# Head norms of a hybrid decoder layer: sums of squares as four column strips instead of two full matmuls, and two inverse products put into one PSUM bank

## The chip, the cores and the metric

One Trainium2 chip; the program runs on one of its cores. The metric is the device time of one execution in microseconds (us), lower is better. The engines are named as in the profile: PE is TensorE (matmuls), PEld its weight loads, DVE is VectorE, ACT is ScalarE, POOL is GpSimd, and SP is the queue from which nearly all DMAs are issued.

## The reference, cut to what matters

One decoder layer, 2048 tokens, width 1024, all in float32. A combined projection feeds two groups of four heads of width 128: gated DeltaNet heads ("g") and HGRN2 heads ("h"). Every head's output is normed over its 128 channels and gated; then come the output projection, an MLP and a gated embedding, each with RMSNorms.

```
def gated_head_norm(o, w, z):
    o = o * lax.rsqrt(jnp.mean(o * o, axis=-1, keepdims=True) + EPS)
    return o * w.astype(jnp.float32) * jax.nn.silu(z)
...
        o_a = gated_delta_rule_chunked(q_a, k_a, v_a, g_dec, beta)
        o_a = gated_head_norm(o_a, gdn_norm[i], z_gdn)
...
        o_b = hgrn2_chunked(jax.nn.silu(q_hg), k_b, i_hg, log_f)
        o_b = gated_head_norm(o_b, hgrn_norm[i], g_hg)
```

The chunked delta rule solves a triangular system per chunk of the sequence; the kernel builds the inverse of that triangle from 32x32 blocks upward. Two of the products on that way are called `psx5` and `pst5` below.

## The kernel before, in words

Channels stand on the 128 partitions and tokens in the free dimension. The tokens go in four quarters `q` of 512 (`QT`), each of four chunks of 128. The large products keep float32 accuracy by splitting both operands into two parts of type fp32r and adding three products of the parts, each a 128x512 matmul.

The first stage (projections and mixers) runs over `works`: for each quarter one small projection (`ab`) and 32 projections of 24 matmuls each (8 for each of the four head pairs). A work is cut into three **ticks** of eight 128x512 matmuls (`SPT = 3`), so a head pair spans 24 ticks and a quarter 99. All the small work of the heads hangs on these ticks: a head is a generator, and a table of tick offsets (`A_STEPS` for g heads, `B_STEPS` for h heads, `A_LAST` and `B_LAST` for the last pair) says in which tick, counted from its pair's first work, each step up to the next `yield` is emitted. A half offset (`half()`) is a place in the middle of a tick. PE's order is the order of emission, and in this stage SP's is too, so an SP instruction that waits holds up all that stand behind it. The orders of DVE and ACT are set by the scheduler of the framework.

Inside a head PE runs two kinds of small float32 matmuls between the 128x512 ones: full ones (128x128 weights, 128 columns moving: `psa`, `psb`, `psc`, transposes `t_`) and **strips** (`strip`, 32 weight columns at `tile_position=(0, 32 g)`, four of which fill the array side by side: `psp`, `psx`, `pst`, `psd`, `at_all`, the small ones on `of_h` and `of_g`). A float32 matmul stands in the trace as two records, an fp32r one as a single record.

The norm of a head (`finish`, then `norm_steps`): ACT squares the output into `osq`, ACT and DVE split that into the two fp32r parts of `hl`, PE multiplies both by a matrix of ones (two 128x512 matmuls into one bank, `nrm`), so every row of the bank holds the sums; ACT copies row 0 out (1x512), and one row goes to DRAM (`sd`), back as 128x4 (`m`), through DVE and POOL (the -0.5 power), to DRAM (`rd`), and back spread over all partitions (`rsb`). DVE scales the output (`og`) and SP stores it (`mixd`). There are 32 such norms, 16 of g and 16 of h heads. `norm_steps` also serves the four embedding norms (`nrm_e`).

The PSUM pool `pp` of the mixers has three banks that all these small products take in turn.

Of the kernel before, what the change touches and what calls it, by code (L numbers as in the profile page):

```python
# [10 lines left out]
F32 = mybir.dt.float32  # L11
# [3 lines left out]
AF = mybir.ActivationFunctionType  # L15
# [5 lines left out]
P = 128  # L21
# [3 lines left out]
QT = 512  # L25
NQ = T // QT
NC = QT // P
# [4 lines left out]
SB = 32  # L32
# [22 lines left out]

A_STEPS = ((3, 6, 7, 8, 9, 10, 12, 14) + tuple(range(16, 24)) + (24, 26, 28, 30, 32, 34, 36)
           + tuple(o for c in range(38, 54, 4) for o in (c, c + 1.5, c + 2.5))
           + (53, 55, 57, 59, 60, 61, 65, 66))
I_STEPS = (22,)
B_STEPS = (24, 26, 28, 30, 32, 34, 36, 38, 40, 42, 44, 45, 46, 48, 50, 52, 53, 54, 58, 59)  # L60


A_AHEAD = (-12, -6)
# [2 lines left out]
A_FIRST = (3, 7, 8, 8, 9, 10, 12, 14) + tuple(range(16, 24)) + (24, 26, 29, 32, 34, 36, 37)  # L66

A_LAST = (A_STEPS[:16] + (24, 25, 27, 28, 29, 30, 31) + tuple(range(32, 44))
          + (44, 47, 49, 50, 51, 52, 54, 55))
B_LAST = tuple(range(24, 34)) + (35, 36, 37, 39, 41, 42, 43, 44, 46, 47)  # L70
LAST = 44


# [23 lines left out]
def trunk(ctx, tc, x, xT, pT, vecs, w_in, w_ab, gdn_a_log, gdn_dt_bias, w_out, w_up, w_down,  # L97
          w_ple, w_gate, consts, out):
    nc = tc.nc
    V, S, G, PE = nc.vector, nc.scalar, nc.gpsimd, nc.tensor  # L100
# [36 lines left out]
    def col(r):  # L137
        return cols[:, r : r + 1]
# [27 lines left out]
    ones = cp.tile([P, P], F32R, name="ones")  # L166
# [4 lines left out]
    def rsqrt(v):  # L171
        G.tensor_tensor(v, v, mhalf, ALU.pow)

    def split(t, eng, raw):

        S.activation(t[:, 0], raw, AF.Copy)  # L176
        eng.tensor_tensor(t[:, 1], raw, t[:, 0], ALU.subtract)  # L177
# [56 lines left out]
    def squares(acc, src, k, name, eng=V):  # L234

        if acc is None:
            acc = st.tile([P, QT], F32, tag="acc", name=f"acc_{name}", bufs=3)
            S.activation(acc, src, AF.Square)
        else:
            turns[0] += 1  # L240
            if pair[0] and turns[0] % 2:
                sq = st.tile([P, QT], F32, tag="late", name=f"sq_{name}_{k}")
            else:
                sq = st.tile([P, QT], F32, tag="sq", name=f"sq_{name}_{k}", bufs=1)
            S.activation(sq, src, AF.Square)  # L245
            eng.tensor_tensor(acc, acc, sq, ALU.add)  # L246
        return acc
# [7 lines left out]
    def spread_load(rd, name, pool=None, tag="rsb", bufs=2):  # L255
        rsb = (pool or st).tile([P, QT], F32, tag=tag, name=f"rsb_{name}", bufs=bufs)
        nc.sync.dma_start(rsb, rd.broadcast_to([P, QT]))
        return rsb
# [15 lines left out]
    yod = {q: [dr.tile([P, QT], F32, name=f"yod{q}_{d}") for d in range(KD)] for q in (0, 2, 3)}  # L274
    ple_r = [None] * NQ

    def norm_steps(acc, scale, eps, name, done, pool=None):

        hl = st.tile([P, 2, QT], F32R, tag="hl", name=f"hl_{name}", bufs=1)
        split(hl, V, acc)  # L280
        yield
        ps = bank(f"nrm_{name}", pool or pp)
        PE.matmul(ps, ones, hl[:, 0, :], start=True, stop=False)
        PE.matmul(ps, ones, hl[:, 1, :], start=False, stop=True)
        row = acc[0:1, :]
        S.activation(row, ps[0:1, :], AF.Copy)
        sd = dr.tile([1, QT], F32, name=f"sd_{name}")
        nc.sync.dma_start(sd, row)
        yield
        m = sm.tile([P, NC], F32, tag="m", name=f"m_{name}")  # L290
        nc.sync.dma_start(m, sd.rearrange("o (p n) -> (o p) n", n=NC))
        yield
        V.tensor_scalar(m, m, scale, eps, ALU.mult, ALU.add)
        rsqrt(m)
        yield
        rd = dr.tile([1, QT], F32, name=f"rd_{name}")
        nc.sync.dma_start(rd.rearrange("o (p n) -> (o p) n", n=NC), m)
        done(rd)
# [91 lines left out]
    with ExitStack() as ectx:  # L390
        es = ectx.enter_context(tc.tile_pool(name="es", bufs=1))
        with tc.manual_schedule(engines={mybir.EngineType.SP, mybir.EngineType.Activation, mybir.EngineType.DVE}):
# [44 lines left out]
            done = []  # L437
# [23 lines left out]
    with mixers as mctx:  # L461
# [145 lines left out]
        def finish(q, h, pso, zt, extra, eps, n):  # L607

            og = st.tile([P, QT], F32, tag="late", name=f"og_{n}")
            sq = st.tile([P, QT], F32, tag="acc", name=f"osq_{n}", bufs=3)  # L610
            S.activation(sq, pso, AF.Square, scale=P ** -0.5)
            V.tensor_tensor(og, pso, zt, ALU.mult)
            if extra is not None:
                V.tensor_tensor(sq, sq, extra, ALU.add)
            rd = []
            yield from norm_steps(sq, 1.0, eps, n, rd.append)
            yield
            rsb = spread_load(rd[0], n)
            yield
            V.scalar_tensor_tensor(og, og, col(R_GNORM if h < 4 else R_HNORM), rsb, ALU.mult, ALU.mult)  # L620
            yield
            nc.sync.dma_start(mixd[q][h], og)
# [10 lines left out]
        def gdn_mixer(q, h, live):  # L633

            n = f"g{q}_{h}"
# [8 lines left out]
            both = sm.tile([P, 2, NC], F32, tag="tail", name=f"tail_{n}")  # L644
# [41 lines left out]
            for c in range(0, NC, 2):  # L686
                ps = (of_h if c else of_g).rearrange("p (a b i) -> p a b i", a=2, b=2)
# [44 lines left out]
            for part_m, part_i in ((slice(SB // 4, SB // 2), slice(SB // 2, SB)), (slice(0, SB // 4), slice(0, SB))):  # L732
                width = part_i.stop - part_i.start
                t = fix[:, :, :width]
# [36 lines left out]
            def pair_bank(name):  # L771
                return bank(f"{name}_{n}", pp)[:, : QT // 2].rearrange("p (a i) -> p a i", a=2)

            def half_bank(name):
                return bank(f"{name}_{n}", pp)[:, : QT // 4].rearrange("p (a i) -> p a i", a=2)

            psp = half_bank("psp5")
            for p in range(2):  # L780
                for g in range(NB):
                    strip(g, psp[rows_of(g), p, rows_of(1 - g % 2)], um[5][:, p, rows_of(g)],
# [2 lines left out]
                S.activation(part[5][rows_of(g), :, rows_of(g ^ 1)], psp[rows_of(g), :, rows_of(0 if g % 2 else 1)],  # L785
                             AF.Copy)
            yield
            psx, pst = half_bank("psx5"), half_bank("pst5")
            for p in range(2):
                for g in range(NB):  # L790
                    strip(g, pst[rows_of(g), p, rows_of(g % 2)], part[5][:, p, rows_of(g)],
# [9 lines left out]
            psp = pair_bank("psp6")  # L801
# [352 lines left out]
        with tc.manual_schedule(engines={mybir.EngineType.SP}):  # L1154
# [5 lines left out]
            for j, (name, key, src, q, h, then, g, b) in enumerate(works):  # L1160
# [3 lines left out]
                ps = bank(f"mm_{name}")  # L1164
# [25 lines left out]
    pp = ctx.enter_context(tc.tile_pool(name="pq", bufs=4, space=PSUM))  # L1190
# [264 lines left out]
    for j, (q, d) in enumerate(order):  # L1455
# [32 lines left out]
        if j in held:  # L1488
            ps = held.pop(j)
        elif order[j] == TOGETHER[0]:  # L1490
# [5 lines left out]
            ps = held.pop(j)  # L1496
        else:
            ps = bank(f"mmo_{q}_{d}", pp)
# [3 lines left out]
        acc = square_sums[q] = squares(square_sums[q], ps, d, f"o{q}")  # L1502
# [403 lines left out]
    for half in range(2):  # L1906
# [4 lines left out]
        for d in range(KD):  # L1911
# [6 lines left out]
            for s, q in enumerate(qs):  # L1918
# [3 lines left out]
                ps = bank(f"mmg_{q}_{d}", pp)  # L1922
# [4 lines left out]
                t = es.pop((q, d))  # L1927
# [55 lines left out]
```

## Time and profile before

| what | value |
|---|---|
| median of 3 runs | 2637.18 us (2633.91 to 2642.8) |
| the profiled execution | 2643.16 us, span 2641.4 us |
| PE, DVE, ACT, POOL busy | 2601.6, 1964.7, 1464.2, 137.2 us |
| granted clock of TensorE | 1.00 |
| first stage in the trace | to about 1060 us of the span |

The busy time of PE counts a matmul until its modelled end, which lies behind the start of the next one, so the distance between starts, not the duration, tells what a matmul costs in a stream. "Idle before" an instruction starts at that modelled end too. A `PE ... <- X` in the views below means that PE's idle time ended when X released it.

### The profile page before, as it was taken

What the parts mean: (1) busy time and instruction counts of PE and PEld (TensorE: products, weight loads), DVE (VectorE), ACT (ScalarE), POOL (GpSimd) and SP (SyncE); (2) the same over time, 40 slices, a digit from 0 to 9 for tenths busy, and PEclk for the clock granted to TensorE, in tenths of its full rate; (3) what the DMA queues carried; (4) which work ended last, traced back from release to release, by engine and by line L of the source; (5) the groups of instructions that cost most, each with busy time, mean ns of one, the idle gap of its engine ahead of it and who ended that gap; (6) DMA issues with size and microseconds to landing.
All of it is one profiled execution on the core that took longest, in us unless ns stands there. A gap on an engine that the chain in (4) does not pass through costs nothing.

```text
span 2641.4 us, 43911 instructions
## 1 busy us (share of the span) xinstructions
PE 2601.6 (98%) x15593; PEld 2143.3 (81%) x15593; DVE 1964.7 (74%) x4032; ACT 1464.2 (55%) x2991; POOL 137.2 (5%) x147
## 2 busy tenths in 40 slices
PE   8999999999999999999999999999999999999999
PEld 5788788878878888787888888888888888888887
DVE  7788777776777777578988778767877765477776
ACT  7675655465555555566566465555455465565322
POOL 0000000000000000110000000001000001101000
PEclk9999999999999999999999999999999999999999
DMA  8777777767767675774675576665644375677664
GB/s 278 276 266 259 253 264 247 239 215 253 242 201 250 228 233 165 222 211 142 216 230 185 183 231 221 214 211 187 220 151 168 138 245 188 200 253 251 204 218 134
DMA packets 267788, 573.87 MB, mean 217 GB/s; under 512 B 55578, under 2 KB 60152, under 8 KB 250416
## 3 DMA queue, kind: packets, MB, share of 16 engines
q1 hardware_dynamic: 265264, 566.86, 64.5%
q0 software_dynamic: 2304, 4.20, 0.9%
q8 instruction: 123, 2.02, 0.3%
q14 instruction: 97, 0.79, 0.1%
HBM read 410.57 MB, written 160.37 MB: 216 GB/s over the span
## 4 chain that ended last, share of the span: by engine, by line
PE 76%; DMA 10%; DVE 7%; ACT 3%; issue 3%; SPq 1%; POOL 0%; DVEq 0%; ACTq 0%; POOLq 0%
PE d L1208 23%; PE u L1208 23%; PE mm L1174 17%; PE mmg L1208 7%; DMA cache_in<-w 2%; DMA sys_g<-ud_g 1%; PE mme L203 1%; DMA ud_g<-u_g 1%; DMA raw_out<-in_w_out_dram 1%; DMA mixT<-mixd 1%; DMA xs<-in_x_dram 1%; DMA yod<-yo 1%; DVE w L177 1%; DVE pr_g L744 0%; DMA wd<-in_w_down_dram 0%
## 5 line engine op out<-in xcount | busy, mean ns | idle before, releaser
L1174 PE MATMUL mm<-xt,w 128*128 128x512 f32 x3072 | 785.6, 401 | 2.6 <-DVE acc_vg L569 1.3
L1174 PEld LDWEIGHTS mm<-xt,w 128*128 128x128 f32 x3072 | 552.6, 188 | 109.1 <-ACT w L176 1.7
L1208 PE MATMUL d<-db,da 128*128 128x512 f32 x2688 | 612.8, 389 | 0.0
L1208 PE MATMUL u<-t,wu 128*128 128x512 f32 x2604 | 591.2, 389 | 0.0
L1208 PEld LDWEIGHTS d<-db,da 128*128 128x128 f32 x2688 | 504.5, 188 | 104.8
L1208 PEld LDWEIGHTS u<-t,wu 128*128 128x128 f32 x2604 | 488.7, 188 | 101.5
L230 DVE TENSOR_TENSOR db<-db 128x512 fp32r<-128x512 f32 x224 | 159.5, 712 | 62.0 <-ACT db L229 60.9
L1606 DVE TENSOR_TENSOR u<-u,u 128x512 f32<-128x512 f32 x224 | 150.5, 683 | 52.7 <-PE u L1208 51.2
L229 ACT ACTIVATE db<-db 128x512 fp32r<-128x512 f32 x224 | 140.9, 629 | 69.1 <-DMA db<-hid 66.7
L1208 PE MATMUL mmg<-h2T,wg 128*128 128x512 f32 (+1 forms) x792 | 174.7, 383 | 0.0
L1208 PEld LDWEIGHTS mmg<-h2T,wg 128*128 128x128 f32 x792 | 145.5, 188 | 29.1
L1649 ACT ACTIVATE u<-u 128x512 f32<-128x512 f32 x128 | 80.8, 631 | 155.0 <-DVE u L1606 154.5
L177 DVE TENSOR_TENSOR da<-da 128x512 fp32r<-128x512 f32 x128 | 94.5, 738 | 91.8 <-ACT da L176 89.9
L176 ACT ACTIVATE da<-da 128x512 fp32r<-128x512 f32 x128 | 80.6, 630 | 129.0 <-DMA da<-sumd 110.9
L1208 PE MATMUL mmo<-mixT,w_out 128*128 128x512 f32 x600 | 138.9, 391 | 3.6 <-DVE w_out L177 1.6
L1208 PEld LDWEIGHTS mmo<-mixT,w_out 128*128 128x128 f32 x600 | 112.1, 188 | 29.4 <-DVE w_out L177 2.9
L176 ACT ACTIVATE wu<-a 128x512 fp32r<-128x512 f32 x124 | 75.1, 623 | 53.3 <-DMA a<-in_w_up_dram 51.5
L177 DVE TENSOR_TENSOR wu<-a,wu 128x512 fp32r<-128x512 f32 x124 | 86.0, 695 | 8.0 <-ACT wu L176 7.5
L177 DVE TENSOR_TENSOR da<-dr,da 128x512 fp32r<-128x512 f32 x96 | 68.3, 711 | 22.4 <-ACT da L176 21.0
L1650 ACT ACTIVATE u<-u 128x512 f32<-128x512 f32 x128 | 80.4, 628 | 3.0
L246 POOL TENSOR_TENSOR acc_y<-acc_y,sq_y 128x512 f32<-128x512 f32 x28 | 37.6, 1341 | 759.9 <-ACT sq_y L245 759.9
L176 ACT ACTIVATE da<-dr 128x512 fp32r<-128x512 f32 x96 | 60.5, 630 | 29.4 <-DMA dr<-in_w_down_dram 21.1
(401 smaller groups left out, 3677.2 us busy)
## 6 DMA issues: line engine op xcount, KB each, us to landing
w<-cache_in SPq DMA_DIRECT2D x96, 1024.0 KB
db<-hid SPq DMA_DIRECT2D x224, 256.0 KB
cache_in<-w SPq DMA_DIRECT2D x32, 1024.0 KB
hid<-u SPq DMA_DIRECT2D x128, 256.0 KB
da<-sumd SPq DMA_DIRECT2D x128, 256.0 KB
a<-in_w_up_dram SPq DMA_DIRECT2D x124, 256.0 KB
hid<-ht SPq DMA_DIRECT2D x96, 256.0 KB
dr<-in_w_down_dram SPq DMA_DIRECT2D x96, 256.0 KB
```

The costliest lines, as they stand in the source:

```text
L176: S.activation(t[:, 0], raw, AF.Copy)
L177: eng.tensor_tensor(t[:, 1], raw, t[:, 0], ALU.subtract)
L203: PE.matmul(ps, a, b, start=i == 0, stop=i == n - 1)
L229: S.activation(t[:, 0], plain(t), AF.Copy)
L230: V.tensor_tensor(t[:, 1], plain(t), t[:, 0], ALU.subtract)
L246: eng.tensor_tensor(acc, acc, sq, ALU.add)
L1174: PE.matmul(ps, *terms[i], start=i == 0, stop=i == nt - 1)
L1208: PE.matmul(ps, a, b, start=start, stop=stop)
L1606: V.tensor_tensor(c[new], c[old], ps, ALU.add)
L1649: S.activation(c[k], c[k], AF.Relu)
L1650: S.activation(c[k], c[k], AF.Square)
```

## The change

The 32 head norms no longer split the squares. `norm_in_strips` takes the unsplit float32 squares: for each of the four chunks of 128 tokens one matmul with 32 columns of ones as weights, at column strip `c`, so that the sums of chunk `c` stand in partitions 32c to 32c+31 of a 128x128 area. ACT copies that area (128x128) in place of a row of 512; the DMA `sd` takes one partition of each strip (4x128). The rest of the chain is as before. The embedding norms keep the old way (`norm_whole`).

The chain has one step more, since `sd` is now issued in a tick of its own, and the tables move it. Counted in ticks of its pair, a g head now runs squares at 53, matmuls and copy at 56, `sd` 57, `m` 59, power 61, `rd` 62, `rsb` 63, scaling 67, `mixd` 68 (before: 53, all of 55, 57, 59, 60, 61, 65, 66). An h head: 46, 52, 53, 55, 57, 58, 59, 63, 64 (before: 46, all of 48, 50, 52, 53, 54, 58, 59). The last pair ends in the same ticks as before.

Second, `psx5` and `pst5`, two half-used banks before, become two areas of one bank (`half_banks`).

```
-           + (53, 55, 57, 59, 60, 61, 65, 66))
+           + (53, 56, 57, 59, 61, 62, 63, 67, 68))
...
-    def norm_steps(acc, scale, eps, name, done, pool=None):
+    def norm_in_strips(acc, name):
+
+        yield
+        ps = bank(f"nrm_{name}", pp)[:, :P]
+        for c in range(NC):
+            PE.matmul(ps[c * SB : (c + 1) * SB, :], ones.bitcast(F32)[:, :SB], acc[:, blk(c)], start=True, stop=True,
+                      tile_position=(0, c * SB))
+        S.activation(acc[:, :P], ps, AF.Copy)
+        sd = dr.tile([1, QT], F32, name=f"sd_{name}")
+        yield
+        nc.sync.dma_start(sd.rearrange("o (c n) -> (o c) n", n=P), acc[::SB, :P])
+        yield
+        return sd
+
+    def norm_whole(acc, name, pool):
 
         hl = st.tile([P, 2, QT], F32R, tag="hl", name=f"hl_{name}", bufs=1)
         split(hl, V, acc)
...
+    def norm_steps(acc, scale, eps, name, done, pool=None, strips=False):
+
+        sd = yield from norm_in_strips(acc, name) if strips else norm_whole(acc, name, pool)
...
-            yield from norm_steps(sq, 1.0, eps, n, rd.append)
+            yield from norm_steps(sq, 1.0, eps, n, rd.append, strips=True)
...
-            def half_bank(name):
-                return bank(f"{name}_{n}", pp)[:, : QT // 4].rearrange("p (a i) -> p a i", a=2)
+            def half_banks(name, count):
+                t = bank(f"{name}_{n}", pp)[:, : count * QT // 4]
+                return t.rearrange("p (m a i) -> m p a i", m=count, a=2)
 
-            psp = half_bank("psp5")
+            psp = half_banks("psp5", 1)[0]
...
-            psx, pst = half_bank("psx5"), half_bank("pst5")
+            both = half_banks("psx5", 2)
+            psx, pst = both[0], both[1]
```

PE's queue at the norm of the first h head (quarter 0, head 0), before; `mm` are the projections, `x3` counts matmuls in a row:

```order
L1174 MATMUL mm_0_2_1914<-xt_1_481,w_0_2_1744 128x512 x2
L1174 MATMUL mm_0_2_1914<-xt_2_498,w_0_2_1744 128x512 x2
L283 MATMUL nrm_h_0_1927<-hl_h_0_1879,ones 128x512
L284 MATMUL nrm_h_0_1927<-hl_h_0_1879,ones 128x512
L1174 MATMUL mm_0_2_1914<-xt_2_498,w_0_2_1744 128x512
```

The norm stood by itself between projections. The same norm on PE now:

```order
L1195 MATMUL mm_0_2_1986<-xt_5_547,w_0_2_1829 128x512
L282 MATMUL nrm_h_0_2008<-osq_h_0_1875,ones 32x128 x4
L650 MATMUL of_h<-att_h_1_1925,one 32x4x16 x4
L650 MATMUL at_all<-hb_h_1_1926,qk_h_1_1658 32x2x16 x16
L1195 MATMUL mm_0_2_1986<-xt_5_547,w_0_2_1829 128x512 x2
```

It has moved by four ticks and stands directly ahead of the first strips of the next h head. PE's queue at the norm of the first g head, before (`t_kg` are transposes of the head after next):

```order
L1174 MATMUL mm_0_2_2093<-xt_5_547,w_0_2_1907 128x512
L283 MATMUL nrm_g_0_2144<-hl_g_0_2073,ones 128x512
L284 MATMUL nrm_g_0_2144<-hl_g_0_2073,ones 128x512
L599 MATMUL t_kg_2_2153<-cst,y_kg_2_1990 128x128 x4
L1174 MATMUL mm_0_2_2093<-xt_5_547,w_0_2_1907 128x512 x2
```

There it stood ahead of four full float32 matmuls. The same norm on PE now (`psx` is the name of both inverse products):

```order
L1195 MATMUL mm_0_2_2082<-xt_7_566,w_0_2_1903 128x512 x3
L282 MATMUL nrm_g_0_2163<-osq_g_0_2062,ones 32x128 x4
L650 MATMUL psx_g_1_2170<-xt_g_1_1963,part_586 32x32 x4
L650 MATMUL psx_g_1_2170<-part_586,xt_g_1_1963 32x32 x2
L650 MATMUL psx_g_1_2170<-xt_g_1_1963,part_586 32x32 x4
L650 MATMUL psx_g_1_2170<-part_586,xt_g_1_1963 32x32 x2
L650 MATMUL at_all<-qk_h_1_1658,keys_h_1_2_2113 32x2x16 x8
```

It has moved by one tick, to the head of the run of strips with the next g head's inverse products. Of the 32 norms 23 stand like these two, in a run of strips between the projections' matmuls; 7 stand alone between projections (mostly those of a quarter's fourth pair, which the `ab` projection shifts against the next quarter), and 2 stand beside full 128x128 matmuls.

SP's queue around the second pair of quarter 0, before (`raw` and `cache_in` move the projections' weights, `xd` and `xn` carry the inverse's 32x32 blocks to DRAM and back):

```order
L192 DMA cache_in_2683<-w_0_3_2520 128x2048
L288 DMA sd_h_1_2702<-osq_h_1_2647 1x512
L750 DMA xd_g_2_2704<-xs_g_2_2476 128x128
L291 DMA m_h_1_2741<-sd_h_1_2702 128x4
L757 DMA xn_g_2_2744<-xd_g_2_2704 32x4x32 x4
L510 DMA raw_0_3_2762<-in_w_in_dram 128x1024
```

`sd_h` stood ahead of `xd_g`, and `m_h` between `xd_g` and `xn_g`. The same stretch of SP's queue now:

```order
L769 DMA xd_g_2_2691<-xs_g_2_2472 128x128
L776 DMA xn_g_2_2729<-xd_g_2_2691 32x4x32 x4
...
L287 DMA sd_h_1_2778<-osq_h_1_2643 4x128
...
L310 DMA m_h_1_2891<-sd_h_1_2778 128x4
...
L287 DMA sd_g_1_2929<-osq_g_1_2826 4x128
L316 DMA rd_h_1_3000<-m_h_1_2891 128x4
L310 DMA m_g_1_3079<-sd_g_1_2929 128x4
L257 DMA rsb_h_1_3081<-rd_h_1_3000 128x512
L529 DMA raw_0_3_3094<-in_w_in_dram 128x1024
```

`sd_h` and `m_h` have moved behind the inverse's blocks, and `rd_h`, the other head's `m_g` and `rsb_h` now stand in a row ahead of the next transfer of weights.

More of the change, by code (lines that the diff above doesn't have):

```diff
@@ L57 @@
            + tuple(o for c in range(38, 54, 4) for o in (c, c + 1.5, c + 2.5))
-           + (53, 55, 57, 59, 60, 61, 65, 66))
+           + (53, 56, 57, 59, 61, 62, 63, 67, 68))
 I_STEPS = (22,)
-B_STEPS = (24, 26, 28, 30, 32, 34, 36, 38, 40, 42, 44, 45, 46, 48, 50, 52, 53, 54, 58, 59)
+B_STEPS = (24, 26, 28, 30, 32, 34, 36, 38, 40, 42, 44, 45, 46, 52, 53, 55, 57, 58, 59, 63, 64)
 A_AHEAD = (-12, -6)
@@ L68 @@
 A_LAST = (A_STEPS[:16] + (24, 25, 27, 28, 29, 30, 31) + tuple(range(32, 44))
-          + (44, 47, 49, 50, 51, 52, 54, 55))
-B_LAST = tuple(range(24, 34)) + (35, 36, 37, 39, 41, 42, 43, 44, 46, 47)
+          + (44, 46, 47, 49, 50, 51, 52, 54, 55))
+B_LAST = tuple(range(24, 34)) + (35, 36, 37, 38, 39, 41, 42, 43, 44, 46, 47)
 LAST = 44
@@ L289, in norm_steps @@
         yield
+        return sd
+    def norm_steps(acc, scale, eps, name, done, pool=None, strips=False):
+        sd = yield from norm_in_strips(acc, name) if strips else norm_whole(acc, name, pool)
         m = sm.tile([P, NC], F32, tag="m", name=f"m_{name}")
```

## The prediction

> **What bounds the kernel now.** I read the page's first part, then busy time by stage (windows), the groups by line, the waits of PE, and the timeline of PE around norms and strips. Page:
>
> ```profile
> span 2641.4 us, 43911 instructions
> PE 2601.6 (98%) x15593; PEld 2143.3 (81%) x15593; DVE 1964.7 (74%) x4032; ACT 1464.2 (55%) x2991; POOL 137.2 (5%) x147
> PE 76%; DMA 10%; DVE 7%; ACT 3%; issue 3%; SPq 1%; POOL 0%; DVEq 0%; ACTq 0%; POOLq 0%
> L1208 PE MATMUL d<-db,da 128*128 128x512 f32 x2688 | 612.8, 389 | 0.0
> ```
>
> PE is busy for 98% of the span at the granted clock of 1.00, and is most of the chain that ended last. The last row gives the price of a 128x512 matmul in a stream: 612.8 / 2688 = 0.228 us (389 ns is its latency; the next starts 0.228 later). By stage (PE, PEld, DVE, ACT, POOL):
>
> ```profile
> 40.00:1060.00 1020.00, 1003.24 (x8551) 825.97 (x8550) 768.55 (x2176) 597.75 (x1548) 61.15 (x80) 1.00 0.72 239
> 1240.00:2641.00 1401.00, 1396.98 (x6186) 1157.54 (x6184) 1032.69 (x1598) 727.44 (x1212) 58.13 (x44) 1.00 0.61 203
> ```
>
> The change is in the first stage. There PE idles 1020.0 - 1003.2 = 16.8 us, DVE is at 75%, ACT at 59%. So nearly all that the change takes from PE comes off the span, and what it takes from DVE and ACT can be worth at most those 16.8 us, plus 0.389 - 0.228 = 0.16 us per wait, which the modelled end of the matmul before hides. Who ends PE's idle time:
>
> ```profile
> PE of_g L631 <- ACT y_qg L578: 2.6, 3, 1.0
> PE psa_g L818 <- DVE S_g L830: 2.5, 4, 0.9
> PE psp_g L631 <- DMA xn_g<-xd_g: 1.3, 1, 1.3
> PE mm L1174 <- DMA w<-cache_in: 0.4, 1, 0.4
> ```
>
> Small waits on everybody (total us, times, longest): no engine is a second bound here, and the weights come in time.
>
> **The change, part by part.** *The two full matmuls go.* Timeline of PE around one norm (start, length):
>
> ```profile
> 586.36 0.39 PE L283 MATMUL nrm_h<-hl_h,ones 128*128 128x512 f32 x1
> 586.59 0.39 PE L284 MATMUL nrm_h<-hl_h,ones 128*128 128x512 f32 x1
> 586.82 1.08 PE L1174 MATMUL mm<-xt,w 128*128 128x512 f32 x4
> ```
>
> From 586.36 to the next projection at 586.82 it costs 0.46 us, two stream prices of 0.228. All on PE: 32 x 0.456 = **-14.6 us**.
>
> *The strips come.* Four matmuls of 128 moving columns are 8 records of 128 columns in float32. The trace has no strip like it, so I compare two runs of strips that differ by 16 records of 64 columns, the same 1024 record-columns:
>
> ```profile
> 109.97 0.33 PE L631 MATMUL at_all<-qk_h,keys_h 128*32 128x32 f32 x16
> 110.23 0.96 PE L1174 MATMUL mm<-xt,w 128*128 128x512 f32 x3
> ...
> 621.31 0.43 PE L631 MATMUL psd_g<-xt_g,part 128*32 128x64 f32 x16
> 621.56 0.31 PE L631 MATMUL at_all<-qk_h,keys_h 128*32 128x32 f32 x16
> 621.80 1.89 PE L1174 MATMUL mm<-xt,w 128*128 128x512 f32 x7
> ```
>
> The first run lasts 110.23 - 109.97 = 0.26 us, the second 621.80 - 621.31 = 0.49, so 1024 record-columns add 0.23 us inside a run that is there anyway. Below that it can hardly get, since columns have to stream. Above, if the four strips ran one after another at the price of full float32 matmuls,
>
> ```profile
> L950 PE MATMUL pss_h<-v_h,hk_h 128*128 128x128 f32 x128 | 16.9, 275 | 0.0
> ```
>
> 8 x 16.9 / 128 = 1.06 us. The `psd` row is a strip and nearer; I take 0.23. 32 x 0.23 = **+7.4 us**.
>
> The Trainium skill speaks against this price: in "TensorE: Matmul & The Clock Gate", Part 3 ("What overlaps and what doesn't"), weight loads overlap running matmuls only where the row groups differ, and these strips all use all rows. By that page's load price (columns / 1.2, in ns; section "LDWEIGHTS") eight loads of 32 columns would lie open, an estimate of 8 x 27 ns = 0.21 us per norm or 6.8 us in all, and the sum below would be -1.6 in place of -8.4. The trace does not bear it out for these strips: the 16 `psd` records, each with a weight load of its own, cost 0.23 us together.
>
> *Entering and leaving strips* costs time of its own:
>
> ```profile
> 604.64 2.20 PE L1174 MATMUL mm<-xt,w 128*128 128x512 f32 x9
> 606.77 0.33 PE L631 MATMUL psp_g<-xn_g,um 128*32 128x32 f32 x16
> ...
> 607.16 2.09 PE L1174 MATMUL mm<-xt,w 128*128 128x512 f32 x8
> 609.09 0.60 PE L599 MATMUL t_kg<-cst,y_kg 128*128 128x128 f32 x4
> ```
>
> The nine projections ahead take 606.77 - 604.64 = 2.13 us against 9 x 0.228 = 2.05, the eight behind 1.93 against 1.82: 0.08 and 0.11. The 0.26 us of the shortest run above holds 16 records of 32 columns, half of 1024, so 0.12 for columns and 0.14 fixed. A visit to strips costs 0.08 + 0.11 + 0.14 = 0.33 us, whoever is in it. The 23 norms that join a run pay nothing of it. The 7 that stand alone pay it, and the 2 beside full matmuls too, for those do not run in strips: 9 x 0.33 = **+3.0 us**. (The Trainium skill, "TensorEngine Tiling (Array Packing)", section "Tiling Modes", says that a change of tiling mode drains the engine; it gives no price.) PE's own part is -14.6 + 7.4 + 3.0 = -4.2 us. A norm that joins gains 0.456 - 0.23 = 0.23 us; one alone loses 0.33 + 0.23 - 0.456 = 0.10.
>
> *The split goes from ACT and DVE, and the row copy becomes a block copy:*
>
> ```profile
> L177 DVE TENSOR_TENSOR hl_h<-osq_h,hl_h 128x512 fp32r<-128x512 f32 x16 | 10.9, 682 | 0.0
> L176 ACT ACTIVATE hl_h<-osq_h 128x512 fp32r<-128x512 f32 x16 | 10.1, 630 | 0.4
> L286 ACT ACTIVATE osq_h<-nrm_h 1x512 f32<-1x512 f32 x16 | 9.3, 583 | 8.5 <-PE nrm_h L284 8.4
> L669 ACT ACTIVATE kt_g<-t_kg,tail_g 128x128 f32<-128x128 f32 x64 | 18.0, 369 | 0.0
> ```
>
> DVE loses 32 x 0.68 = 21.9 us. ACT loses 32 x (0.63 + 0.58) and gains 32 copies of 128x128 at the 0.37 us of the nearest row, so -27 us. Neither bounds the stage; only PE's waits count. First the norms' own, which have no counterpart now, since `osq` is finished three to six ticks ahead:
>
> ```profile
> L284 PE MATMUL nrm_g<-hl_g,ones 128*128 128x512 f32 x16 | 6.7, 419 | 0.6 <-DVE hl_g L177 0.4
> L283 PE MATMUL nrm_g<-hl_g,ones 128*128 128x512 f32 x16 | 6.3, 396 | 0.4 <-ACT hl_g L176 0.4
> ...
> PE nrm_g L284 <- DVE hl_g L177: 0.4, 2, 0.2
> PE nrm_g L283 <- ACT hl_g L176: 0.4, 1, 0.4
> ```
>
> 1.0 us idle; 16 x (419 - 389) + 16 x (396 - 389) ns = 0.6 us by which the waiting ones are longer than the 389 ns of a stream; and 0.16 us behind the modelled end of the matmul before for the three waits that the last rows count, 0.5: **-2.1 us**. Then waits at the end of a full DVE queue. One is seen in DVE's timeline:
>
> ```profile
> 522.76 0.68 DVE L177 TENSOR_TENSOR hl_h<-osq_h,hl_h 128x512 fp32r<-128x512 f32 x1
> ...
> 529.45 0.34 DVE L830 SCALAR_TENSOR_TENSOR S_g<-S_g,cd_g,psc_g 128x128 f32<-128x128 f32 x1
> ```
>
> DVE works without a pause from one to the other, and PE waits for that `S_g`:
>
> ```profile
> 529.84 0.49 PE L818 MATMUL psa_g<-S_g,y_kg 128*128 128x128 f32 x2 [0.62 <-DVE S_g L830]
> ```
>
> Without the 0.68 us in front nearly all of this wait goes. In the whole stage `S_g` stalls PE four times (2.5 us). What is late next is ACT (`y_qg`, 2.6 us), which the split's end may help as well, and other DVE work. All other waits of the stage are the bounds: from -16 (they all go) to +8 (as much again as half of them arises, since 0.75 us scalings `og` and the scheduler's order now fall elsewhere). I take **-2.1 us**, three stalls of about 0.7, the row seen.
>
> *The chain's shift.* Nothing but `mixd` hangs on a norm's end, and the last pair ends in its old ticks, so the delay of two to five ticks is free; its cover is the distance to the output projection. On SP the change takes a wait away: `sd` was issued in the tick of its matmul and waited for ACT,
>
> ```profile
> SPq L288 <- ACT osq_h L286: 49.7, 15, 8.3
> SPq L291 <- DMA sd_g<-osq_g: 22.6, 10, 5.1
> SPq L257 <- DMA rd_h<-m_h: 30.2, 10, 5.1
> SPq L197 <- PE mm L1174: 230.2, 56, 8.2
> ```
>
> with `xd_g` queued behind it, which PE waits for once (1.3 us, above). It adds one: `m_g` and `rsb_h` wait in a row ahead of a transfer of weights. That is covered, since the weights' transfer waits for its buffer anyway, 230.2 / 56 = 4.1 us on average. I count both at zero; the range carries them (-1.3, and the slow rival below).
>
> *One bank for two products* changes no instruction of PE. A copy now may wait for both products, some 0.03 us apart, a tick ahead of its use: zero.
>
> **Sum:** -4.2 - 2.1 - 2.1 = -8.4 us. The profiled execution took 2643.16 us (span 2641.4 and 1.8 around it); it would take 2634.8. It lies 6.0 above the median of the runs, so I put the same 8.4 us on the median: 2637.18 - 8.4 = **2628.8 us**. That is 0.32%; about 0.3% (7.9 us) is what a measurement of this kernel can tell from no change, so the forecast lies just past that line.
>
> **The rivals.**
> *Waits stay:* PE saves its -4.2 us and perhaps the norms' own waits, but the stalls on DVE and ACT come back elsewhere. For it: the waits above are spread over many causes. Against it: 22 and 27 us less work. Between -2 and -6, some 2633 us. Chance 0.24, within 0.3%.
> *More relief:* DVE and ACT queues shorten so that a further third of the idle 16.8 us goes: -8.4 - 5 = -13.4, 2624 us. For it: saturated DVE queues as the one shown. Chance 0.24, faster.
> *Strips gain little:* every norm pays its own visit (32 x 0.10 = +3.3 in place of -4.2, sum -0.9, 2636 us), or its weight loads lie open. The loads of `psd` are busy for 4.4 us in 256:
>
> ```profile
> L631 PEld LDWEIGHTS psd_g<-xt_g,part 128*32 128x32 f32 x256 | 4.4, 109 | 6.3 <-issue 3.2 <-ACT part L804 1.2 <-ACT e_g L655 0.4
> ```
>
> That is 17 ns each, 8 x 17 = 0.14 us per norm, 4.4 us in all, sum -4.0, 2633 us. PE's order excludes the first for the 23 norms that join; against the second speaks the 0.23 us of the `psd` run, which holds such loads. (That the loads lie open would follow from the page of the Trainium skill named above, "TensorE: Matmul & The Clock Gate", Part 3.) Chance 0.04, within 0.3%.
> *Slower, by SP:* the two waits in a row cost 3.0 + 2.3 = 5.3 us on average (30.2 / 10, 22.6 / 10), 1.2 more than the weights' cover of 4.1. If the weights then come 1.2 us late for PE in all 16 pairs, that is +19, sum +10.8, 2648 us. It decides only from where the cover is used up; PE waited 0.4 us in all for weights. Chance 0.06.
>
> The forecast itself has 0.42, from -6 to -10.5, 2626.7 to 2631.2, with its middle just past the line: 0.23 faster, 0.19 the same. Faster 0.23 + 0.24 = 0.47, same 0.19 + 0.24 + 0.04 = 0.47, slower 0.06. The range takes in the waits that stay and the further relief, and the few us by which runs of this kernel differ: 2619 to 2638.
>
> **What would show it.** In the profile after: `nrm` strips in runs that are 0.23 us longer than the same runs before; a norm alone taking about 0.56 us with its borders; PE busy in the first stage down by some 4 to 5 us; no wait on `hl`; DVE about 22 and ACT about 27 us less busy; fewer waits on `S_g`; no new wait on `w<-cache_in`. It is wrong if a joined norm costs over 0.4 us, if new waits on DVE or ACT sum to over 5 us, or if PE waits for weights.

## The result, and the profile after

The kernel after takes 2642.63 us (median of 20 runs, 2638.79 to 2648.04), the one before 2639.36 in the same comparison (20 runs): ratio 1.0014, 95% interval 1.0008 to 1.002, so 3.7 us slower where 8.4 us less were forecast, and above the range of 2619 to 2638 us. The profiled execution took 2639.23 us (span 2637.5), one of the kernel's quickest; that of before (2643.16) was longer than any of its 20 runs. The two spans therefore must not be subtracted, and before and after were each profiled a second time (below). From the page of after:

```profile
span 2637.5 us, 44250 instructions
PE 2600.6 (99%) x15785; PEld 2140.7 (81%) x15785; DVE 1946.2 (74%) x4000; ACT 1435.2 (54%) x2959; POOL 136.7 (5%) x147
```

DVE is 18.5 us less busy than before and ACT 29.0 us. PE has 192 matmul records more (32 norms, 8 instead of 2) and as many weight loads, so 384 more instructions. The first stage by windows (PE, PEld, DVE, ACT, POOL):

```profile
40.00:1060.00 1020.00, 1006.60 (x8777) 826.75 (x8776) 754.16 (x2150) 572.31 (x1521) 62.18 (x81) 1.00 0.72 240
```

PE is 3.4 us busier in this fixed window than before, since the window now holds more of the output projection: the last projection matmul starts at 1006.3 us here and at 1014.1 in the first profile of before. What the first stage gained can't be read from it.

The prices of the strips came out as forecast. PE's timeline around the first h norm after, and the same run of strips in the second profile of before:

```profile
164.38 0.43 PE L282 MATMUL nrm_h<-osq_h,ones 128*32 128x128 f32 x8
164.63 0.29 PE L650 MATMUL of_h<-att_h,one 128*32 128x64 f32 x8
164.74 0.48 PE L650 MATMUL at_all<-hb_h,qk_h 128*32 128x32 f32 x32
165.15 1.19 PE L1195 MATMUL mm<-xt,w 128*128 128x512 f32 x4
```

```profile
164.06 0.32 PE L631 MATMUL of_h<-att_h,one 128*32 128x64 f32 x8
164.19 0.48 PE L631 MATMUL at_all<-hb_h,qk_h 128*32 128x32 f32 x32
164.60 1.19 PE L1174 MATMUL mm<-xt,w 128*128 128x512 f32 x4
```

With the norm the run lasts 165.15 - 164.38 = 0.77 us, without it 0.54: the joined norm costs 0.23. A norm alone, after:

```profile
1062.40 1.97 PE L1229 MATMUL mmo<-mixT,w_out 128*128 128x512 f32 x8
1064.30 0.42 PE L282 MATMUL nrm_g<-osq_g,ones 128*32 128x128 f32 x8
1064.66 2.57 PE L1229 MATMUL mmo<-mixT,w_out 128*128 128x512 f32 x10
```

0.36 us for itself and 1.90 - 1.82 = 0.08 at its entry; with the 0.11 of the prediction at its exit that is 0.55 (forecast 0.56). Waits of PE in the first stage after (total us, times, longest) name no `hl` any more, but others stand in its place:

```profile
PE psc_g L849 <- ACT w_g L846: 1.6, 2, 1.0
PE of_g L650 <- ACT y_qg L597: 1.5, 2, 1.2
PE psa_g L839 <- DVE pr_g L763: 1.4, 3, 0.7
...
PE psa_g L839 <- DVE S_g L851: 1.0, 2, 0.8
PE mm L1195 <- DMA w<-cache_in: 0.9, 2, 0.7
```

The stalls on `S_g` fell from four (2.5 us; three and 1.8 in the second profile) to two (1.0). The one that the prediction shows behind a split, 0.62 us, is 0.26 now, the last row here:

```profile
518.80 0.49 PE L839 MATMUL psa_g<-S_g,y_kg 128*128 128x128 f32 x2 [0.75 <-DVE S_g L851]
528.18 0.49 PE L839 MATMUL psa_g<-S_g,y_kg 128*128 128x128 f32 x2 [0.26 <-DVE S_g L851]
```

The first row, 0.75 us, was 0.86 before. Here no split was in the way: two instructions ahead of `S_g`, DVE waits for a load (before, then after):

```profile
518.35 0.75 DVE L1095 SCALAR_TENSOR_TENSOR raw_xt<-raw_xt,cols,rsb_x 128x512 f32<-128x512 f32 x1 [1.27 <-DMA raw_xt<-in_xT_dram]
```

```profile
517.52 0.75 DVE L1116 SCALAR_TENSOR_TENSOR raw_xt<-raw_xt,cols,rsb_x 128x512 f32<-128x512 f32 x1 [0.45 <-DMA raw_xt<-in_xT_dram]
```

All of PE's waits that this view names from 40 to 1012 us sum to 12.3 us (second profile of after 13.2; before 14.9 and 10.0).

The surprise lies behind the first stage, in work that the change does not touch. From the last projection matmul to the end it takes 1631.2 us (second profile 1630.9) against 1627.2 (1626.8) before. Waits of PE from 1060 to 1240 us, after and then before:

```profile
PE mmo L1229 <- DVE w_out L177: 3.3, 2, 2.1
PE u L1229 <- ACT w_u L176: 2.3, 1, 2.3
```

```profile
PE mmo L1208 <- DVE w_out L177: 1.6, 3, 0.7
PE u L1208 <- ACT w_u L176: 0.9, 1, 0.9
```

The second pair of rows is the first product `u` of the MLP. PE's timeline there, after and in the second profile of before (start, length; idle time in brackets):

```profile
1216.80 0.73 PE L1229 MATMUL u<-t,w_u 128*128 128x512 f32 x2 [2.35 <-ACT w_u L176]
1217.94 2.93 PE L1229 MATMUL u<-t,w_u 128*128 128x512 f32 x6 [0.41 <-DVE w_u L177]
1220.67 0.57 PE L1260 MATMUL nrm_o<-hl_o,ones 128*128 128x512 f32 x1
```

```profile
1214.84 0.73 PE L1208 MATMUL u<-t,w_u 128*128 128x512 f32 x2 [0.88 <-ACT w_u L176]
1215.98 1.66 PE L1208 MATMUL u<-t,w_u 128*128 128x512 f32 x6 [0.41 <-DVE w_u L177]
1217.48 0.39 PE L1239 MATMUL nrm_o<-hl_o,ones 128*128 128x512 f32 x1
```

The wait is 1.47 us longer, and the six matmuls behind it take 1220.67 - 1217.94 = 2.73 us in place of 1.50: they run at about half speed, and the granted clock shows it. Windows from 1200 to 1260 us, after and the first profile of before:

```profile
1200.00:1260.00 60.00, 57.24 (x245) 46.66 (x244) 53.75 (x88) 43.62 (x75) 0.00 (x0) 0.97 0.40 131
```

```profile
1200.00:1260.00 60.00, 58.73 (x259) 47.99 (x258) 55.61 (x91) 39.57 (x70) 0.00 (x0) 1.00 0.38 128
```

### The profile page after: what moved, and what is told of

Its sections match the earlier page's. It is cut to its first block, busy times and chain, and to the rows that moved or that the text cites. A ratio compares the mean times of both kernels' runs of the same rounds, so it can differ in the third digit from the quotient of the medians.

```text
span 2637.5 us, 44250 instructions
## 1 busy us (share of the span) xinstructions
PE 2600.6 (99%) x15785; PEld 2140.7 (81%) x15785; DVE 1946.2 (74%) x4000; ACT 1435.2 (54%) x2959; POOL 136.7 (5%) x147
## 4 chain that ended last, share of the span: by engine, by line
PE 71%; issue 4%; DMA 4%; DVE 3%; ACT 2%; SPq 0%; POOL 0%; DVEq 0%; POOLq 0%; ACTq 0%
PE d L1229 23%; PE u L1229 23%; PE mm L1195 11%; PE mmg L1229 7%; PE mmo L1078 1%; PE mme L203 1%; PE mmo L1229 1%; DMA sys_g<-ud_g 1%; DMA mixT<-mixd 1%; DMA h1d<-yo 0%; PE psa_g L839 0%; DMA ud_g<-u_g 0%; PE of_h L982 0%; PE pss_h L971 0%; PE of_h L981 0%
```

## The experiments

"Rest" below is the span minus the start of the last projection matmul, in one profile. All ratios are against runs of before made beside them.

**Repeats, the tables, the bank.** `before_again` and `after_again` are the two kernels unchanged. `strips_old_ticks` has the strips but before's tables, with `sd` in the tick of its matmuls:

```
-            + (53, 56, 57, 59, 61, 62, 63, 67, 68))
+            + (53, 55, 57, 59, 60, 61, 65, 66))
...
         S.activation(acc[:, :P], ps, AF.Copy)
         sd = dr.tile([1, QT], F32, name=f"sd_{name}")
-        yield
```

`two_banks` gives the two inverse products a bank each again:

```
-            both = half_banks("psx5", 2)
-            psx, pst = both[0], both[1]
+            psx, pst = half_banks("psx5", 1)[0], half_banks("pst5", 1)[0]
```

> The kernel before once more, for the spread of its runs and a second profile. Both theories: ratio to itself 1.000, within 0.1%. Theory 'given back behind the first stage' (PE gains 8 us in the first stage, then arrives at the output projection before its operands, waits there, and each wait of over 2 us halves PE's clock for some 3 us): granted clock 0.999 to 1.000 in all runs, since its waits there are under 1.4 us; first stage ends (last projection matmul) near 1014 us. Theory 'the first stage is not shorter in a usual run' (the profile of the changed kernel was one of its best runs, that of the kernel before one of its worst): the first stage ends near 1006 to 1010 us in this profile.

> The changed kernel once more. Both theories: ratio 1.001 to 1.002. 'Given back behind': the first stage ends near 1006 us again, the loss lies between there and the first products of the MLP (1.0 + 3.0 us and more), clock 0.997 to 0.998. 'First stage not shorter': the first stage ends near 1010 to 1014 us, with waits on DVE, ACT or DMA that the first profile did not have.

> Strips and one bank as changed, but the norms' steps in the ticks of the kernel before, sd in the tick of its matmul. Most norms then stand alone or beside full matmuls: 28 x 0.10 - 4 x 0.23 = about +2 us on PE against before, less 2 us of waits on the split. 'Given back behind': first stage as long as before (0 to -2), ratio 0.999 to 1.001, clock above 0.998. 'First stage not shorter': the shift of the chain is what brings new waits there, so this kernel has none of them: ratio 0.998 to 1.000.

> The changed kernel with the two inverse products in two banks again. My prediction priced the shared bank at zero: ratio within 0.05% of the changed kernel's (1.001 to 1.002) by both theories. If the shared bank makes PE or the copies wait, this kernel is faster than the changed one by 1 to 5 us.

Measured: `before_again` 2637.81 us, ratio 1.0000 (0.9991 to 1.0009), rest 1626.8; `after_again` 2642.40, 1.0012 (1.0003 to 1.0021), rest 1630.9; `strips_old_ticks` 2651.96, 1.0056 (1.0044 to 1.0069), rest 1630.9; `two_banks` 2642.26, 1.0018 (1.001 to 1.0027), rest 1630.9. So the 4 us of the rest return in a second profile, and the shared bank is worth nothing that shows. The last projection matmul starts at 1007.3 us in `before_again` and at 1006.8 in `after_again`, so each of the two theories was half right: before's usual first stage is not the long one of its first profile, and the loss lies behind that stage. Strips without the shift are dearer by about 0.4% than with it, though both theories had put them at 0.998 to 1.001: a miss.

**Does the last pair reorder VectorE?** In the output projection DVE's queue after holds the last pair's `og_g` ahead of a split of `w_out` that PE waits for (the 2.1 us above). Four kernels. `last_whole`: the last pair keeps whole norms and its old ticks. `last_strips`: only the last pair has strips. `shift_whole`: after's tables with whole norms everywhere. `rsb_later`: one row is asked for a tick later, which puts the split ahead of `og_g`.

```
last_whole:   strips=(q, h % 4) != (NQ - 1, 3)      and before's A_LAST, B_LAST
last_strips:  strips=(q, h % 4) == (NQ - 1, 3)      and before's A_STEPS, B_STEPS
shift_whole:  sd = yield from norm_whole(acc, name, pool, late=strips)    (late: a yield ahead of the sd store)
rsb_later:    A_LAST ends 44, 46, 47, 49, 50, 51, 53, 55, 56    (after: 52, 54, 55)
```

> The last pair's two norms go back to split squares and full matmuls at the ticks of before; the fifteen other pairs keep strips and the shifted ticks. Theory "the last pair's norm reorders VectorE": with it og_g of the last pair stands behind two w_out splits again, so the 2.0 to 2.1 us wait of mmo on a VectorE w_out split and the half-speed matmuls behind it go; from the last projection matmul to the end it takes 1627 to 1629.5 us (after 1631, before 1627), and the time is 2639 to 2641. Rival "the cost comes from the strips of the other pairs": the rest stays at 1631 and the time at 2642 to 2643. Rival "first u product alone": the wait on w_out goes but the 2.0 to 2.3 us wait of u on a ScalarE w_u split stays, and the rest is 1629.

> Strips for the last pair's two norms alone; all other pairs as in before (split squares, full matmuls, old ticks). Theory "the last pair's norm reorders VectorE": the first stage is before's, the wait of mmo on a VectorE w_out split of about 2 us appears, the rest behind the last projection matmul is 1629 to 1631 us and the time 2639.5 to 2642. Rival "the cost comes from the strips of the other pairs": rest 1627, time 2637 to 2638.

> After's tick tables (chain a tick or more later) with before's split squares and full matmuls, the matmuls and the store of the row at the strips' ticks. Theory "the shift costs nothing and the strips only trade": time within 2 us of before, 2636 to 2640, rest behind the first stage 1627. Rival "the later chain is what ate the relief of the first stage": the first stage is 3 us or more longer than before's, time 2641 to 2645.

> After with the last pair's row rsb_g asked for one tick later (A_LAST ends 53, 55, 56 instead of 52, 54, 55), which puts the second w_out split ahead of og_g in VectorE's queue, as in before. Theory "VectorE waits at og_g for rsb_g with a w_out split behind it": the 2 us wait of mmo goes, the matmuls behind it run at 227 ns, rest 1627 to 1629, time 2638.5 to 2640.5. Rival "that order is worth nothing": rest 1631, time 2642 to 2643.

Measured: `last_whole` 2638.65 us, ratio 1.0000 (0.9988 to 1.0012), rest 1626.3, u's wait 0.9. `last_strips` 2639.39, 1.0002 (0.9992 to 1.0013), rest 1628.0, with the 2.1 us wait on `w_out`. `rsb_later` 2642.75, 1.0012 (1.0001 to 1.0023), rest 1632.1, u's wait 2.2. `shift_whole` 2645.92, 1.0025 (1.0014 to 1.0037), rest 1626.7.

`last_whole` alone would have carried the theory. The two others bring it down: `last_strips` has the wait and keeps most of before's rest, and `rsb_later` has before's order at that place and keeps after's. And all kernels with a long rest have u's long wait. `shift_whole` answers another question: the later chain, with the split still in it, costs 0.25%, and its rest is before's, so the cost is in the first stage.

**Where u's wait comes from.** PE waits for ScalarE's split of `w_u`, which stands in the queue behind work that waits for loads of `b` (parts of the hidden state that DVE then scales, 256 KB each). SP issues a pair of them at the same place in both kernels, 18.6 us ahead of the first `u`. After: SP's issue, DVE's wait for the landing, and the DMA queues between 1190.3 and 1194.7 us:

```profile
1190.27 0.92 SPq L1384 DMA_DIRECT2D b<-h1d  x2
```

```profile
1194.70 0.75 DVE L1385 SCALAR_TENSOR_TENSOR b<-b,cols,rn 128x512 f32<-128x512 f32 x1 [1.41 <-DMA b<-h1d]
```

```profile
q8 instruction: 1, 0.02, 2.3%
```

Second profile of before:

```profile
1189.80 0.92 SPq L1363 DMA_DIRECT2D b<-h1d  x2
```

```profile
1192.75 1.41 DVE L1364 SCALAR_TENSOR_TENSOR b<-b,cols,rn 128x512 f32<-128x512 f32 x2
```

4.43 us from issue to use after, at most 2.95 before. In between, after has one transfer of kind "instruction" on queue q8, and before has none. It begins at 1190.97 by its record, moves 16 KB and lasts 1.6 us (2.3% of 16 engines' 4.4 us). The pages count such transfers (packets, MB), after and before:

```profile
q8 instruction: 125, 2.05, 0.3%
```

```profile
q8 instruction: 123, 2.02, 0.3%
```

2 x 15785 records of PE by 125 are 253 per transfer, 2 x 15593 by 123 are 254: so these look like the fetches of PE's own instructions, one for every 250 or so, some 30 us apart behind the first stage. The change adds 384 instructions, one and a half fetches, so behind the first stage every fetch should stand half a period elsewhere; near the first `u` it went from -4.3 to -17.9 us, 13.6 of 30. By this theory the number of PE's instructions ahead of the place is all that matters, and it can be changed with nothing else: small matmuls in PE's idle time at the start.

```
         ps = bank(f"mme_{q}_{d}")
+        for _ in range(16 if (q, d) == (0, 0) else 0):
+            PE.matmul(ps[:, :SB], ones, ones[:, :SB], start=True, stop=True)
         project(...)
```

> After with 16 matmuls of ones by 32 columns put ahead of the first matmul, where TensorE idles until 7.42 us; each is a weight load and a matmul, so 32 more instructions on TensorE and nothing else. Theory "instruction fetch": the 16 KB fetch of TensorE's queue that began 17.9 us before the first u product, between the loads of b and their landing, moves to about 21.5 us before it; the loads of b are on time (VectorE's wait for them under 0.2 us instead of 1.0 to 1.4), the wait of u on the ScalarE w_u split falls from 2.0 to 2.4 us to 0.9, the matmuls behind it run at 227 ns, and from the last projection matmul to the end it takes 1628 to 1629.5 us instead of 1631; time 2639.5 to 2641. Rival "VectorE's and ScalarE's order behind the first stage": nothing there changes, so 1631 and 2642 to 2643.

> Before with 58 such small matmuls ahead of the first matmul (116 instructions on TensorE). Theory "instruction fetch": the fetch that began 4.3 us before the first u product moves to about 17.5 us before it, among the loads of b; these are 0.8 to 1.4 us late, u waits 2.0 to 2.4 us instead of 0.9, and the part behind the first stage takes 1628.5 to 1630 us instead of 1627; time 2638.5 to 2640. Rival "order": 1627 and before's 2637 (up to 1 us more where the small matmuls delay the start).

And as a control, with a second phase:

> Control: before with the same 16 small matmuls. By the theory "instruction fetch" its fetch moves from 4.3 to about 7.9 us before the first u product, where nothing lands that u waits for: behind the first stage 1626.5 to 1627.5 us, time within 1.5 us of before. Rival "the small matmuls themselves help, in any kernel" (an earlier clock, other phases in the first stage): 2 us or more faster than before, as after_pad16 was (4 us).

> After with 28 small matmuls: the fetch comes about 22.7 us before the first u product, the loads of b are on time (no wait of VectorE for them at the third pair), u waits 0.9 us for its ScalarE split (1.3 with 16), rest 1625.5 to 1626.5 us. Time 2634 to 2636.5 if what the change saves in the first stage does not hang on this phase; 2638 or more if the 4 us of after_pad16 were luck of the first stage.

Measured: `after_pad16` 2635.35 us, ratio 0.9985 (0.9976 to 0.9994); `after_pad28` 2636.21, 0.9994 (0.9985 to 1.0003); the control `before_pad16` 2639.14, 1.0007 (0.9995 to 1.0018); `before_pad58` 2648.81, 1.0037 (1.0025 to 1.0049), of which 7.5 us are its later start (first `ab` matmul at 46.85 against 39.38 us), which its expected 2638.5 to 2640 did not hold. `after_pad16` is 4 us quicker than expected, with the fetch at -20.0 and not at -21.5. In both padded kernels of after the last projection matmul starts at 1006.3 and 1007.1, as in after: their gain lies behind the first stage. DVE and PE in `before_pad58`, where the fetch was moved among the loads:

```profile
1204.42 1.41 DVE L1366 SCALAR_TENSOR_TENSOR b<-b,cols,rn 128x512 f32<-128x512 f32 x2 [1.70 <-DMA b<-h1d]
```

```profile
1226.50 0.73 PE L1210 MATMUL u<-t,w_u 128*128 128x512 f32 x2 [2.59 <-ACT w_u L176]
1227.65 2.59 PE L1210 MATMUL u<-t,w_u 128*128 128x512 f32 x6 [0.41 <-DVE w_u L177]
```

and in `after_pad28`, where it was moved out:

```profile
1192.54 1.41 DVE L1387 SCALAR_TENSOR_TENSOR b<-b,cols,rn 128x512 f32<-128x512 f32 x2
```

```profile
1214.62 0.73 PE L1231 MATMUL u<-t,w_u 128*128 128x512 f32 x2 [0.87 <-ACT w_u L176]
1215.77 1.65 PE L1231 MATMUL u<-t,w_u 128*128 128x512 f32 x6 [0.41 <-DVE w_u L177]
```

All kernels, in us (the fetch nearest to the pair of `b`, counted from the first `u`; the pair is issued at -18.6 and -18.1, used from -15.6):

| kernel | fetch starts | `b` late | u waits | 100 `u` from the first | rest |
|---|---|---|---|---|---|
| before (two profiles) | -4.3, -4.3 | 0, 0 | 0.9, 0.9 | 25.0, 25.0 | 1627.2, 1626.8 |
| shift_whole | -3.6 | 0 | 0.9 | 25.0 | 1626.7 |
| last_strips | -7.0 | 0 | 0.9 | 25.0 | 1628.0 |
| before_pad16 | -8.0 | 0 | 0.9 | 25.0 | 1625.4 |
| last_whole | -15.2 | 0 | 0.9 | 25.0 | 1626.3 |
| two_banks | -16.1 | 1.27 | 2.3 | 28.0 | 1630.9 |
| before_pad58 | -16.4 | 1.70 | 2.6 | 28.4 | 1631.8 |
| after (two profiles) | -17.9, -18.0 | 1.41, 0.99 | 2.4, 2.0 | 27.9, 26.1 | 1631.2, 1630.9 |
| rsb_later | -18.0 | 1.23 | 2.2 | 27.9 | 1632.1 |
| strips_old_ticks | -18.7 | 0.77 | 1.7 | 25.8 | 1630.9 |
| after_pad16 | -20.0 | 0.38 | 1.3 | 25.4 | 1626.2 |
| after_pad28 | -22.7 | 0 | 0.9 | 25.0 | 1627.2 |
| h_strips (below) | -26.7 | 0 | 0.9 | 25.0 | 1627.3 |
| g_strips (below) | -27.5 | 0 | 0.8 | 24.9 | 1626.0 |

Where a fetch starts between -18.7 and -16.1 the pair comes 0.8 to 1.7 us late, in every kernel; at -20.0 it is still 0.4 late, further off never. Moved in, the fetch spoils before; moved out, it heals after. And the fetch goes with the count: 32 instructions more moved it from -4.3 to -8.0 in before, 3.7 of 30 us for 32 of 254. In which way the 16 KB hold up the load was not traced. `last_whole` was healed by the 24 PE instructions that its two whole norms save. The stretch of 100 `u` accounts for 2.9 of the 4 us in the first profile of after and for 1.1 in the second. What else lengthens the rest lies between the last projection and the first `u` (202.2 to 203.5 us in the kernels with a late pair by 0.8 us or more, 199.7 to 201.6 in the others) and in the second profile also behind the 100; it goes with the same phase but was not traced to one wait.

**Which chain gives the relief back?** In the first stage, take every visit of PE to small matmuls between two projections, and subtract the shortest visit with matmuls of the same shapes in any of these kernels. The sum of these excesses, for visits of the serial inverse (`psa`, `psb`, `psc`) and for all others:

| | serial visits | others |
|---|---|---|
| before's tables and norms (two profiles, pad16, pad58) | 10.2, 6.9, 8.7, 8.3 | 11.7, 9.9, 9.5, 9.7 |
| after's (two profiles, pad16, pad28) | 14.0, 12.8, 14.8, 13.2 | 6.6, 7.0, 6.5, 7.0 |
| shift_whole | 15.6 | 7.4 |
| strips_old_ticks | 14.8 | 12.6 |
| two_banks | 9.7 | 13.0 |
| last_whole, rsb_later | 14.6, 14.1 | 6.6, 8.1 |
| last_strips | 8.8 | 9.5 |

From before to after the others lose 3.4 us on average and the serial visits gain 5.2. The second column does not follow the chain's place alone: `strips_old_ticks` has 14.8 without the shift, and `two_banks`, which shifts as after does, has 9.7 with 13.0 beside it. What after and its variants share is the sum of the two columns: 19.8 to 27.4 us, against 16.8 to 21.9 in before, and nowhere the 4.2 us less that were forecast. `g_strips` and `h_strips` change one kind of head each (`strips=h < 4` or `strips=h >= 4`, and the tables of the other kind as before).

> Strips and the later ticks for the gated delta rule's norms alone (suffix _g); the other heads' norms stay whole at before's ticks. Theory "the later chain hands its relief to the serial inverse" (the excess of visits with psa, psb and psc over their shortest was 6.6 to 10 us in before, 12.6 to 15.3 with both chains later): if the _g chain does it, that excess is 12 or more here and the first stage as in after; if the _h chain does it, 7 to 10 here and the first stage is 2 to 4 us shorter than before's (last projection matmul at 1003 to 1006), time 2634 to 2637.

> The counterpart: strips and later ticks for the other heads' norms alone (suffix _h, 4 to 5 ticks later); the _g norms stay whole at before's ticks. If the _h chain fills the serial visits, their excess is 12 or more here and the time 2639 to 2643; if the _g chain does it, 7 to 10, the last projection matmul at 1003 to 1006 and the time 2634 to 2637.

Measured: `g_strips` 2635.32 us, ratio 0.9991 (0.9982 to 0.9999), serial 10.9, others 7.7, last projection matmul at 1011.1 in its one profile (2638.85 us, a long one). `h_strips` 2654.17, 1.0056 (1.0041 to 1.007), serial 24.9, others 6.3, last projection matmul at 1023.8. PE's waits in the first stage of `h_strips`:

```profile
PE at_all L934 <- DVE acc_vg L589: 5.2, 4, 2.9
PE psa_g L839 <- DVE S_g L851: 4.9, 6, 1.7
...
PE psc_g L849 <- ACT w_g L846: 3.0, 4, 1.3
```

By the expectations that would name the h chain, but both runs miss a part of them: `h_strips` is 11 us above its 2639 to 2643, and the last projection matmul of `g_strips` is 5 us behind its 1003 to 1006. And `h_strips` does something else as well. With the h chain moved and the g chain not, DVE waits much longer for the spread rows `rsb` with which it scales. DVE's waits from 40 to 1012 us, `h_strips` and then after:

```profile
DVE og_g L639 <- DMA rsb_g<-rd_g: 22.6, 14, 4.8
DVE og_h L639 <- DMA rsb_h<-rd_h: 13.7, 9, 4.7
```

```profile
DVE og_g L639 <- DMA rsb_g<-rd_g: 6.4, 4, 2.1
DVE og_h L639 <- DMA rsb_h<-rd_h: 5.5, 6, 2.2
```

(19.7 us together in the first profile of before, 14.3 in the second.) The longest wait of PE on `S_g` in `h_strips` is one of these handed on, DVE and then PE:

```profile
327.60 0.75 DVE L639 SCALAR_TENSOR_TENSOR og_g<-og_g,cols,rsb_g 128x512 f32<-128x512 f32 x1 [4.76 <-DMA rsb_g<-rd_g]
```

```profile
328.67 0.49 PE L839 MATMUL psa_g<-S_g,y_kg 128*128 128x128 f32 x2 [1.72 <-DVE S_g L851]
```

So an h chain four to five ticks later, beside a g chain that stays, costs 0.56%, in part because DVE stands still at a scaling. That the h chain does the same beside a later g chain, as in after, is not shown: there these waits are shorter than in before. Which work fills the serial visits of after stays open.

## Why the prediction was wrong, point by point

- **Full matmuls gone, strips, visits: -4.2.** Right, for the size. The joined norm costs 0.23, the lone one 0.55; the shortest visits sum to some 10 us more than in before (nearly the same count), against 14.6 saved: about -4.4. That 0.23 is a floor, since "columns have to stream", was not shown: 1024 columns in 0.23 us are twice the rate of a 128x512 matmul in a stream (512 in 0.228), so strips already overlap. The sentence on open weight loads (the Trainium skill, "TensorE: Matmul & The Clock Gate", Part 3) would, by the prediction's estimate, have added 0.21 us to each; the trace of after does not show them.
- **Relief of waits: -2.1 and -2.1.** Failed. The waits on `hl` are gone and the visits outside the inverse lost 3.4 us, but the serial visits took 5.2: +1.8 in place of -4.2. Two steps behind it were wrong. One is "three stalls of about 0.7, the row seen": the stalls on `S_g` fell by 1.5 us (0.8 between the second profiles), since only two of the four stood behind a split, 0.62 and 0.64 us, and of the row seen 0.26 are left; the two others (0.86 and 0.39) stood behind a load. And other waits took the place of what went. The other step is "so the delay of two to five ticks is free": I asked who needs the norm's end, and not what DVE, ACT and SP do in the ticks into which the chain moves. `shift_whole`, 0.25% slower, is the price of that step with the split kept. What fills the serial visits of after is not shown.
- **SP, the bank: 0 and 0.** Nothing against them: PE waited 0.9 us for weights (1.4 in the second profile) against 0.4, and `two_banks` differs from after by less than either interval.
- **What was missing.** No term stood for the place of PE's instruction fetches. It was worth 4 to 5 us behind the first stage, as much as the largest net term. With the fetch moved out, after is quicker than before (0.9985) or the same (0.9994, with 1 inside its interval); beside a control of before with 16 small matmuls (2639.14), after with 28 takes 2636.21 in the same comparison. So without the fetch the change is worth some 2 to 4 us, still short of 8.4.
- **Sum.** -4.4 + 1.8 + 4 = +1.4 us from the traces; the runs say +3.7. From the first `ab` matmul to the last projection matmul four profiles each take 970.2 us on average with before's norms (967.9 to 974.6) and 966.6 with after's (965.8 to 967.8), with and without small matmuls, 3.6 less, which is near the -2.6 of the first two terms. The 2 us that are left are not explained: both profiled executions of after (2639.23 and 2639.55) are 3 us quicker than its median run.
- Of the rivals, "waits stay" was the nearest for the first stage; none held the fetch. "Slower, by SP" had the sign with a wrong cause.

The quickest versions are after with 16 small matmuls (0.9985) and `g_strips` (0.9991): both beat before, by little, where after stands at 1.0012 to 1.0014.

## What to carry to other kernels

When a change moves instructions of a full engine, look for a difference in stages that it does not touch, by the distance from a landmark to the end, before explaining anything in the stage that it does. If there is one, count that engine's instructions: a few dozen harmless ones at an idle place are a cheap test of whether a fetch meets a critical load, and an experiment that changes the count by accident can confirm a wrong theory. A chain that nobody waits for is still work on shared queues: before calling a delay free, list what those queues do in the ticks where it lands. And before counting several waits as one kind, look behind each of them: two of four here hung on a load.

## What the hardware showed unexpectedly

Near the loads of the table a 16 KB instruction fetch lasted 0.9 to 1.6 us by its record (up to 3.3 elsewhere in these traces), and a pair of 256 KB loads issued from 2.5 us before to 1.9 us after its start came 0.4 to 1.7 us late. After the waits of 2.2 to 2.6 us ahead of `u` TensorE's next matmuls started about 0.43 us apart instead of 0.23, for some 3 us, so such a wait costs more than its length; after the waits of 0.9 to 2.0 us at the same place they did not. Length alone does not decide it: at the wait for `w_out`, near 1095 us, the matmuls slowed after 1.9 and 2.0 us (`after_pad16`, `after_pad28`) and did not after 2.1 us (`last_strips`). The Trainium skill ("TensorE: Matmul & The Clock Gate", Part 1) has the half clock follow an idle window of some 3.4 us; here these shorter waits sufficed, though not each time.
